# Rotary embedding over 16 heads: a skipped block of no-ops, and other cuts of the first load and the last stores

## The chip, the cores and the metric

The kernel runs on one core of a Trainium2 chip. A core has five engines with instruction streams of their own: TensorE (PE, matrix products, results in PSUM), VectorE (DVE), ScalarE (ACT), GpSimd (POOL) and SyncE (SP, which here only issues transfers). Data moves between the main memory and the on-chip memory (128 partitions) by 16 DMA engines; each has a ring of its own for every queue, and a DMA of 128 partitions is spread over all 16, eight partitions to each. The metric is the device time of one execution in microseconds; a smaller number is better.

## The reference

`x` is 16 x 512 x 1024 in float32 (33.5 MB), `cos` and `sin` are 512 x 32. Every row of 1024 is 16 heads of 64, and each head's two halves are rotated by the row's angles:

```python
x = x.reshape(batch, seq, num_heads, head_dim)
x1, x2 = x[..., :half_dim], x[..., half_dim:]
rotated = concatenate([x1 * cos - x2 * sin, x1 * sin + x2 * cos], axis=-1)
```

So every element is read once and written once: 67.1 MB in all.

## The kernel before

Two batch entries make one tile: 128 partitions, each with R = 8 consecutive rows of the sequence (32 KB). There are NT = 8 such tiles of 4 MB and NB = 5 buffers for them (`xin`), so tiles 5 to 7 reuse the buffers of tiles 0 to 2. A tile is computed in place and stored from its own buffer.

All loads and stores of tiles are issued by SP, on one queue, in this order: the first tile in four pieces of two rows (L64), tiles 1 to 4 whole, stores of tiles 0, 1, 2 (L69, each after its compute), loads of tiles 5, 6, 7 (each after the store that frees its buffer), then stores 3, 4, 5, 6 whole and store 7 in four pieces of two rows. SP is in order: what stands behind a waiting transfer waits too. The two tables go out on ScalarE's queue (sine L73, cosine L74).

At the head, GpSimd builds an identity (`ident`, L80 and L81), VectorE makes `sel` from it (L86 to L88), and TensorE spreads the two tables over 128 partitions with it (L93 to L95) into PSUM: `sns_ps` (minus sine and sine side by side) and `cos_ps`. ScalarE copies `sns_ps` to `sns` (L99), which GpSimd reads, and `cos_ps` to `cost` (L100), which nothing reads.

`compute(t)` is x times cosine plus the swapped halves of x times the signed sine:

- rows 0 and 1 (`PEROWS`): the sine product `B` (L126) is made by GpSimd for row 0 and by VectorE for row 1; VectorE multiplies the row by cosine in place (L136); TensorE adds the two in four chunks of 512 (L141, L142), and ScalarE copies each chunk back into the tile (L143).
- rows 2 and 3, 4 and 5, 6 and 7 (`PAIRS`): GpSimd makes the sine product `T` (L131, two buffers), VectorE makes the cosine product `pp` (L147) and adds the two into the tile (L148).

Each engine's order is the program's order (a manual schedule); semaphores carry what depends on another engine. A load piece is waited for by the instructions that read its rows: L126 and L136 by the first piece, L131 and L147 by the piece that holds their rows. A store piece waits for the instructions that wrote its rows.

Of the kernel before, what the change touches and what calls it, by code (L numbers as in the profile page):

```python
# [7 lines left out]
FP32 = mybir.dt.float32  # L8
# [4 lines left out]
def kernel(  # L13
# [8 lines left out]
    nc = tc.nc  # L22
    P = nc.NUM_PARTITIONS
    batch, seq, dim = x.shape
    nh = num_heads
    hd = dim // nh
    half = hd // 2
# [4 lines left out]
    R = seq // HP  # L32
    NT = batch // BP
    assert HP * R == seq and BP * NT == batch
    NB = 5
    PAIRS = (2, 4, 6)
    PEROWS = (0, 1)

    xv = x.rearrange("b (p r) d -> (b p) (r d)", r=R)
    xv = xv.rearrange("(t p) f -> t p f", p=P)  # L40
    ov = out.rearrange("b (p r) h d -> (b p) (r h d)", r=R)
    ov = ov.rearrange("(t p) f -> t p f", p=P)
# [3 lines left out]
    fixed = ctx.enter_context(tc.tile_pool(name="fixed", bufs=1))  # L46
# [8 lines left out]


    x_tiles = [None] * NT
    Q = 2 * dim

    def load(t, pieces=1):  # L60
        x_tiles[t] = xin.tile([P, R * dim], FP32, name="x_sb")
        n = R * dim // pieces
        for i in range(pieces):
            nc.sync.dma_start(out=x_tiles[t][:, i * n:(i + 1) * n], in_=xv[t][:, i * n:(i + 1) * n])  # L64

    def store(t, pieces=1):
        n = R * dim // pieces
        for i in range(pieces):
            nc.sync.dma_start(out=ov[t][:, i * n:(i + 1) * n], in_=x_tiles[t][:, i * n:(i + 1) * n])  # L69

    load(0, pieces=4)
    tabs = fixed.tile([HP, 2, R * half], FP32, name="tabs")
    nc.scalar.dma_start(out=tabs[:, 1], in_=sinv)  # L73
    nc.scalar.dma_start(out=tabs[:, 0], in_=cosv)  # L74
    for t in range(1, NB):
        load(t)


    ident = fixed.tile([P, P], FP32, name="ident")
    nc.gpsimd.memset(ident, 0.0)  # L80
# [1 line left out]
        out=ident, in_=ident, compare_op=ALU.not_equal, fill=1.0,  # L82
        base=0, pattern=[[-1, P]], channel_multiplier=1,
    )
    sel = fixed.tile([HP, 2, P], FP32, name="sel")
    nc.vector.tensor_copy(out=sel[:, 0, :HP], in_=ident[:HP, :HP])  # L86
    nc.vector.tensor_copy(out=sel[:, 0, HP:], in_=ident[:HP, :HP])
# [3 lines left out]
    cos_ps = ptab.tile([P, R, half], FP32, name="cos_ps")  # L91
# [3 lines left out]
    nc.tensor.matmul(out=cos_ps.rearrange("p r j -> p (r j)"), lhsT=sel[:, 0, :], rhs=tabs[:, 0],  # L95
                     start=True, stop=True)
    sns = fixed.tile([P, R, 2, half], FP32, name="sns")
    cost = fixed.tile([P, R, half], FP32, name="cost")
    nc.scalar.copy(out=sns, in_=sns_ps)  # L99
    nc.scalar.copy(out=cost, in_=cos_ps)  # L100

    def view(ap, r0, n):

        return ap[:, r0 * dim:(r0 + n) * dim]
# [5 lines left out]
    def snsb(tab, r0, n):  # L110
        return bass.AP(tensor=tab.tensor, offset=tab.offset + r0 * hd,
                       ap=[tab.ap[0], [hd, n], [0, nh], [1, hd]])

    def swapped(xt, r0, n):
        return bass.AP(tensor=xt.tensor, offset=xt.offset + r0 * dim + half,
                       ap=[xt.ap[0], [hd, n * nh], [-half, 2], [1, half]])

    def compute(t):
        xt = x_tiles[t]
        ts = {}  # L120
        bs = {}

        for r in PEROWS:
            B = bpool.tile([P, dim], FP32, name="B")
            eng = nc.vector if r == PEROWS[-1] else nc.gpsimd
            eng.tensor_tensor(out=B, in0=swapped(xt, r, 1), in1=snsb(sns_ps if eng is nc.vector else sns, r, 1),  # L126
                              op=ALU.mult)
            bs[r] = B
        for r0 in PAIRS:
            T = tpool.tile([P, 2 * dim], FP32, name="T")  # L130
            nc.gpsimd.tensor_tensor(out=T, in0=swapped(xt, r0, 2), in1=snsb(sns, r0, 2), op=ALU.mult)  # L131
            ts[r0] = T

        for r in reversed(PEROWS):
            xr = view(xt, r, 1)
            nc.vector.tensor_tensor(out=xr, in0=xr, in1=cosb(cos_ps, r, 1), op=ALU.mult)  # L136
            for c in range(2):
                ps = prow.tile([P, dim // 2], FP32, name="ps")
                xc = xr[:, c * dim // 2:(c + 1) * dim // 2]
                bc = bs[r][:, c * dim // 2:(c + 1) * dim // 2]  # L140
                nc.tensor.matmul(out=ps, lhsT=ident, rhs=xc, start=True, stop=False)  # L141
                nc.tensor.matmul(out=ps, lhsT=ident, rhs=bc, start=False, stop=True)  # L142
                nc.scalar.copy(out=xc, in_=ps)  # L143
        for r0 in PAIRS:
            pp = ppair.tile([P, 2 * dim], FP32, name="pp")
            xr = view(xt, r0, 2)
            nc.vector.tensor_tensor(out=pp, in0=xr, in1=cosb(cos_ps, r0, 2), op=ALU.mult)  # L147
            nc.vector.tensor_tensor(out=xr, in0=ts[r0], in1=pp, op=ALU.add)  # L148

    for t in range(NB):  # L150
        compute(t)
        if t < NT - NB:
            store(t)
    for t in range(NB, NT):
        load(t)
    for t in range(NT - NB, NB):
        store(t)
    for t in range(NB, NT):
        compute(t)
        store(t, pieces=4 if t == NT - 1 else 1)  # L160


# [33 lines left out]
```

## Time and profile before

| | |
|---|---|
| time, three runs | 162.82, 162.91, 163.51 us; median 162.91 |
| the profiled execution's own time | 162.99 us |
| its span, first to last instruction | 161.0 us (160.97) |
| VectorE busy | 137.8 us (86%), last instruction ends at 150.6 |
| GpSimd busy | 127.1 us (79%) |
| TensorE busy | 78.3 us (49%), mean granted clock 0.758 |
| ScalarE busy | 21.0 us (13%) |
| moved by DMA | 67.25 MB, 418 GB/s over the span |

Times within a profile count from the span's start. "Granted clock" is the share of TensorE's full speed that its throttle allowed. The page's "slices" cut the span in 40 and give each engine's busy share in tenths. In the DMA view a queue's row has its packets, megabytes, and the time that its packets took as a share of 16 engines' time; packets are counted where they start, so over a short window this can pass 100%. q1 is SP's queue, q10 ScalarE's, q14 that by which engines get their instructions. Behind the DMA view lie the records of single packets (start, length, size, queue); they don't name the DMA engine, but on a full ring each packet starts where the one before it ended, so a ring can be followed by its phase. In the timeline a row is: start, length, engine, line, operation, output<-inputs, forms, count, and in brackets the idle time before it and what ended it. An engine's name with a "q" is its instruction queue; a row "SPq" is the issue of DMAs.

### The profile page before, as it was taken

How to read it: one execution, taken by the hardware profiler on the slowest of the kernel's cores; microseconds unless marked ns; L12 is line 12 of the kernel's file. 1: busy time of each engine (PE TensorE's matmuls, PEld its weight loads, DVE VectorE, ACT ScalarE, POOL GpSimd, SP SyncE). 2: the span in 40 equal slices, each digit the busy share in tenths (PEclk: the TensorE clock that was granted, in tenths of full speed). 3: DMA queues.
4: the chain of work that ended last, by engine and by line, in shares of the span. 5: the costliest groups of instructions: out<-in, count | busy, mean ns of one | idle time of the engine just before them, and what ended most of it. 6: DMA issues, size and time to landing. Idle time of an engine off the chain costs nothing. (4 is left out here: it accounts for less than half of the span.)

```text
span 161.0 us, 581 instructions
## 1 busy us (share of the span) xinstructions
PE 78.3 (49%) x134; PEld 32.3 (20%) x134; DVE 137.8 (86%) x75; ACT 21.0 (13%) x35; POOL 127.1 (79%) x38
## 2 busy tenths in 40 slices
PE   0449900598019910894049700990079803991000
PEld 0223300233014400341024200340034202340000
DVE  1077999999999999999999999999999999999400
ACT  3021210014001210022002300121001400121000
POOL 1079999999998799959995999869995999692000
PEclk9999996569755985589957995699655975598555
DMA  5999999999999999999999999999999999999994
GB/s 181 385 419 480 391 497 415 391 472 440 391 456 456 391 432 480 391 415 489 399 417 472 407 415 464 415 407 472 423 399 456 448 399 456 448 391 417 421 423 187
DMA packets 3329, 67.25 MB, mean 418 GB/s; under 512 B 384, under 2 KB 512, under 8 KB 512
## 3 DMA queue, kind: packets, MB, share of 16 engines
q1 hardware_dynamic: 3168, 67.11, 97.6%
q10 hardware_dynamic: 160, 0.13, 0.3%
q14 instruction: 1, 0.01, 0.0%
HBM read 33.69 MB, written 33.55 MB: 418 GB/s over the span
## 5 line engine op out<-in xcount | busy, mean ns | idle before, releaser
L131 POOL TENSOR_TENSOR T<-x_sb,sns 128x2048 f32<-128x2048 f32 x24 | 108.2, 4526 | 10.5 <-DVE x_sb L148 10.5
L141 PE MATMUL ps<-x_sb,ident 128*128 128x512 f32 x64 | 44.8, 790 | 61.0 <-issue 40.4
L148 DVE TENSOR_TENSOR x_sb<-T,pp 128x2048 f32<-128x2048 f32 x24 | 54.9, 2288 | 3.4 <-POOL T L131 1.0
L147 DVE TENSOR_TENSOR pp<-x_sb,cos_ps 128x2048 f32<-128x2048 f32 x24 | 55.0, 2294 | 0.6
L142 PE MATMUL ps<-B,ident 128*128 128x512 f32 x64 | 40.3, 717 | 0.0
L143 ACT COPY x_sb<-ps 128x512 f32<-128x512 f32 x32 | 18.8, 586 | 117.6 <-PE ps L142 117.6
L141 PEld LDWEIGHTS ps<-x_sb,ident 128*128 128x128 f32 x64 | 15.2, 253 | 83.3 <-issue 80.4
L126 POOL TENSOR_TENSOR B<-x_sb,sns 128x1024 f32<-128x1024 f32 x8 | 18.8, 2346 | 7.6 <-ACT sns L99 7.6
L142 PEld LDWEIGHTS ps<-B,ident 128*128 128x128 f32 x64 | 15.4, 241 | 22.0 <-issue 22.0
L136 DVE TENSOR_TENSOR x_sb<-x_sb,cos_ps 128x1024 f32<-128x1024 f32 x16 | 18.8, 1218 | 0.5
L126 DVE TENSOR_TENSOR B<-x_sb,sns_ps 128x1024 f32<-128x1024 f32 x8 | 9.7, 1217 | 7.0 <-ACT sns L99 7.0
L93 PE MATMUL sns_ps<-tabs,sel 64*128 64x256 f32 x2 | 1.2, 697 | 6.2 <-DMA tabs<-in_sin_dram 6.2
L93 PEld LDWEIGHTS sns_ps<-tabs,sel 64*128 64x128 f32 x2 | 0.5, 310 | 6.1 <-issue 6.1
L99 ACT ACT_TABLE_LOAD x1 | 1.3, 1283 | 1.9 <-issue 1.9
L86 DVE COPY sel<-ident 64x64 f32<-64x64 f32 x1 | 0.2, 185 | 1.3 <-POOL ident L81 1.3
L99 ACT COPY sns<-sns_ps 128x512 f32<-128x512 f32 x1 | 0.6, 586 | 5.0 <-PE sns_ps L94 5.0
L95 PE MATMUL cos_ps<-tabs,sel 64*128 64x256 f32 x2 | 1.2, 711 | 0.0
L94 PE MATMUL sns_ps<-tabs,sel 64*128 64x256 f32 x2 | 1.1, 631 | 0.0
L94 PEld LDWEIGHTS sns_ps<-tabs,sel 64*128 64x128 f32 x2 | 0.7, 334 | 0.2
L95 PEld LDWEIGHTS cos_ps<-tabs,sel 64*128 64x128 f32 x2 | 0.5, 306 | 0.6 <-DMA tabs<-in_cos_dram 0.6
L100 ACT COPY cost<-cos_ps 128x256 f32<-128x256 f32 x1 | 0.4, 373 | 0.5 <-PE cos_ps L95 0.5
L80 POOL MEMSET ident<- 128x128 f32 x1 | 0.2, 204 | 0.3 <-POOLq L177 0.3
(7 smaller groups left out, 1.1 us busy)
## 6 DMA issues: line engine op xcount, KB each, us to landing
x_sb<-in_x_dram SPq DMA_DIRECT2D x7, 4096.0 KB, 29.5
out_dram<-x_sb SPq DMA_DIRECT2D x7, 4096.0 KB, 27.0
x_sb<-in_x_dram SPq DMA_DIRECT2D x4, 1024.0 KB, 8.7
out_dram<-x_sb SPq DMA_DIRECT2D x4, 1024.0 KB, 9.2
tabs<-in_sin_dram ACTq DMA_DIRECT2D x1, 64.0 KB, 5.3
tabs<-in_cos_dram ACTq DMA_DIRECT2D x1, 64.0 KB, 6.7
```

The source lines that it names most:

```text
L93: nc.tensor.matmul(out=sns_ps[:, :, 1, :], lhsT=sel[:, 0, :], rhs=sin3, start=True, stop=True)
L94: nc.tensor.matmul(out=sns_ps[:, :, 0, :], lhsT=sel[:, 1, :], rhs=sin3, start=True, stop=True)
L95: nc.tensor.matmul(out=cos_ps.rearrange("p r j -> p (r j)"), lhsT=sel[:, 0, :], rhs=tabs[:, 0], start=True, stop=True)
L99: nc.scalar.copy(out=sns, in_=sns_ps)
L126: eng.tensor_tensor(out=B, in0=swapped(xt, r, 1), in1=snsb(sns_ps if eng is nc.vector else sns, r, 1), op=ALU.mult)
L131: nc.gpsimd.tensor_tensor(out=T, in0=swapped(xt, r0, 2), in1=snsb(sns, r0, 2), op=ALU.mult)
L136: nc.vector.tensor_tensor(out=xr, in0=xr, in1=cosb(cos_ps, r, 1), op=ALU.mult)
L141: nc.tensor.matmul(out=ps, lhsT=ident, rhs=xc, start=True, stop=False)
L142: nc.tensor.matmul(out=ps, lhsT=ident, rhs=bc, start=False, stop=True)
L143: nc.scalar.copy(out=xc, in_=ps)
L147: nc.vector.tensor_tensor(out=pp, in0=xr, in1=cosb(cos_ps, r0, 2), op=ALU.mult)
L148: nc.vector.tensor_tensor(out=xr, in0=ts[r0], in1=pp, op=ALU.add)
```

## The change

- The first tile is loaded in two pieces, rows 0 and 1 (1 MB) and rows 2 to 7 (3 MB), instead of four of two rows. `load` and `store` now take the rows at which to cut.
- Stores 3, 4, 5 and 6 go out in two halves of four rows (2 MB each) instead of whole, and store 7 in two halves instead of four quarters. Stores 0 to 2 stay whole.
- On VectorE, ahead of its first work, a register is set to 0 and a branch on it skips 60 no-op instructions. In the built program the branch ends a block of instructions on every engine: each has an unconditional branch there (SP between the two pieces of the first load, ScalarE between the sine and the cosine load, GpSimd between L80's memset and L81's select, TensorE ahead of its first matmul), and VectorE has the compare-and-branch, the 60 no-ops and the branch behind them ahead of `sel`. No engine waits for another at these branches.
- The copy of `cos_ps` to `cost` is gone. Before, VectorE's first L136 waited for ScalarE (its copies); now it waits for TensorE.
- Two loads of tiles 3 and 4 had waited on SP for a semaphore of an earlier transfer to come free (for the sine load and for the first piece); with fewer pieces they no longer do.

```diff
+    PAD = 60
...
-    def load(t, pieces=1):
+    def load(t, cuts=(0, R)):
         x_tiles[t] = xin.tile([P, R * dim], FP32, name="x_sb")
-        n = R * dim // pieces
-        for i in range(pieces):
-            nc.sync.dma_start(out=x_tiles[t][:, i * n:(i + 1) * n], in_=xv[t][:, i * n:(i + 1) * n])
+        for a, b in zip(cuts, cuts[1:]):
+            nc.sync.dma_start(out=x_tiles[t][:, a * dim:b * dim], in_=xv[t][:, a * dim:b * dim])
 
-    def store(t, pieces=1):
-        n = R * dim // pieces
-        for i in range(pieces):
-            nc.sync.dma_start(out=ov[t][:, i * n:(i + 1) * n], in_=x_tiles[t][:, i * n:(i + 1) * n])
+    def store(t, cuts=(0, R)):
+        for a, b in zip(cuts, cuts[1:]):
+            nc.sync.dma_start(out=ov[t][:, a * dim:b * dim], in_=x_tiles[t][:, a * dim:b * dim])
 
-    load(0, pieces=4)
+    load(0, cuts=(0, 2, R))
...
+    step = nc.vector.alloc_register("step")
+    nc.vector.reg_mov(step, 0)
+    with tc.If(nc.vector.snap(step) > 0):
+        for _ in range(PAD):
+            nc.vector.nop(hint="pad")
...
-    cost = fixed.tile([P, R, half], FP32, name="cost")
     nc.scalar.copy(out=sns, in_=sns_ps)
-    nc.scalar.copy(out=cost, in_=cos_ps)
...
     for t in range(NT - NB, NB):
-        store(t)
+        store(t, (0, 4, R))
     for t in range(NB, NT):
         compute(t)
-        store(t, pieces=4 if t == NT - 1 else 1)
+        store(t, (0, 4, R))
```

More of the change, by code (lines that the diff above doesn't have):

```diff
@@ L57 @@
     x_tiles = [None] * NT
-    Q = 2 * dim
-    def load(t, pieces=1):
+    def load(t, cuts=(0, R)):
         x_tiles[t] = xin.tile([P, R * dim], FP32, name="x_sb")
-        n = R * dim // pieces
-        for i in range(pieces):
-            nc.sync.dma_start(out=x_tiles[t][:, i * n:(i + 1) * n], in_=xv[t][:, i * n:(i + 1) * n])
-    def store(t, pieces=1):
-        n = R * dim // pieces
-        for i in range(pieces):
-            nc.sync.dma_start(out=ov[t][:, i * n:(i + 1) * n], in_=x_tiles[t][:, i * n:(i + 1) * n])
-    load(0, pieces=4)
+        for a, b in zip(cuts, cuts[1:]):
[4 more added lines that the diff above has]
+    load(0, cuts=(0, 2, R))
     tabs = fixed.tile([HP, 2, R * half], FP32, name="tabs")
```

## Prediction

> **What bounds the kernel now.** I read the page's slices and queue table first, then the DMA view and the busy time by windows at the end, the chain of waits, and the timeline of the first 16 us and of the last tile. First the page (queue; packets, MB, share of 16 DMA engines over the span) and its slices:
>
> ```profile
> DMA  5999999999999999999999999999999999999994
> ...
> q1 hardware_dynamic: 3168, 67.11, 97.6%
> q14 instruction: 1, 0.01, 0.0%
> ```
>
> The transfers, all on one queue, fill the span: 0.976 of 161.0 us. In the packet records the first data packet starts at 1.74 us and the last ends at 159.81, and 97.6% of 160.97 us is 157.1 us, so hardly one microsecond of that stretch is idle. The page's chain of waits follows VectorE to its last instruction at 150.60; what remains, 10.4 us, is the drain of stores. The windows over that drain (DMA share is the last column but one):
>
> ```profile
> core 0: us, PE busy (x) PEld busy (x) DVE busy (x) ACT busy (x) POOL busy (x), PEclk, DMA share, GB/s
> 150.00:156.00 6.00, 0.00 (x0) 0.00 (x0) 0.60 (x1) 0.00 (x0) 0.00 (x0) 0.50 1.00 425
> ...
> 158.40:159.00 0.60, 0.00 (x0) 0.00 (x0) 0.00 (x0) 0.00 (x0) 0.00 (x0) 0.50 0.40 164
> 159.00:159.90 0.90, 0.00 (x0) 0.00 (x0) 0.00 (x0) 0.00 (x0) 0.00 (x0) 0.50 0.09 36
> ```
>
> Full until 158.4, then a tail of a few engines. The packet records show 14 DMA engines finishing at 158.43 to 158.96, one at 159.63, one at 159.81: the end is set by the slowest of 16 rings, each with a fixed share of the bytes. The last one has a history. In the DMA view of 82.0 to 82.3 us a packet of another queue stands in the stream:
>
> ```profile
> q14 instruction: 1, 0.01, 6.4%
> ```
>
> In the records it starts at 82.13 on the ring whose data packet ended at 82.13, takes 309 ns, and the 32 KB packet behind it takes 1745 ns instead of 1213: 0.31 + 0.53 = 0.84 us lost on one ring. Followed by its phase, that ring loses 0.385 us more in a packet at 109.67 (1598 ns), and is the one that ends at 159.81. Without the instruction packet it would have ended by 158.97.
>
> Then the compute at the head (start, length, engine, line, [idle before <- what ended it]):
>
> ```profile
> 8.05 1.22 PE L95 MATMUL cos_ps<-tabs,sel 64*128 64x256 f32 x2
> 8.86 1.22 DVE L126 TENSOR_TENSOR B<-x_sb,sns_ps 128x1024 f32<-128x1024 f32 x1 [6.99 <-ACT sns L99]
> ...
> 10.19 2.35 DVE L136 TENSOR_TENSOR x_sb<-x_sb,cos_ps 128x1024 f32<-128x1024 f32 x2
> 11.22 13.49 POOL L131 TENSOR_TENSOR T<-x_sb,sns 128x2048 f32<-128x2048 f32 x3
> ...
> 15.78 2.29 DVE L148 TENSOR_TENSOR x_sb<-T,pp 128x2048 f32<-128x2048 f32 x1 [1.03 <-POOL T L131]
> ```
>
> From 8.86 on VectorE works nearly without a gap (3.4 us idle at L148 in the whole run, page), so whatever delays the first L148 delays the end of compute by as much. And the last tile:
>
> ```profile
> 145.46 0.59 ACT L143 COPY x_sb<-ps 128x512 f32<-128x512 f32 x1 [1.13 <-PE ps L142]
> ...
> 146.08 2.26 SPq L69 DMA_DIRECT2D out_dram<-x_sb  x3
> 148.31 2.29 DVE L148 TENSOR_TENSOR x_sb<-T,pp 128x2048 f32<-128x2048 f32 x1
> ```
>
> Rows 0 and 1 are ready at 146.05, the last rows at 150.60; the rings are busy with the store before until 148.6 (fast rings) to 150.0 (the slow one). So the stores arrive in time, with 1 to 3 us to spare.
>
> **The change, part by part.**
>
> *Packets.* DMAs on the two queues: 24 before, 24 after. Per ring, 8 KB packets fall from 64 to 8, 8 of 24 KB and 80 of 16 KB come, 32 KB packets fall from 112 to 80. From the DMA view of 152 to 158 us (314 data packets, 101.4% of 16 x 6 us) an 8 KB packet is 310 ns; from that of 15 to 45 (400, 101.5%) a 32 KB one 1218. No 16 or 24 KB packet is in this trace; the straight line between those rows gives 613 and 915. Before 64 x 0.310 + 112 x 1.218 = 156.26 us; after 8 x 0.310 + 8 x 0.915 + 80 x 0.613 + 80 x 1.218 = 156.28. Bounds: at the 32 KB rate 609 ns, at the 8 KB rate 620 for 16 KB, so -0.4 to +0.7 us. I take the line: 0.0.
>
> *The first tile.* Its first piece is as before. The rest was 3 pieces landing at 8.9, 11.3 and 13.8 (issue plus the DMA view's time to landing: 1.16 + 7.7, 1.63 + 9.7, 2.10 + 11.7); now it is one, and lands with the last of those bytes, 13.8. GpSimd's first T (L131) needs rows 2 and 3: 11.22 becomes 13.80, +2.58. It takes 4.54, so VectorE's first L148 starts at 18.36, not 15.78. The later T's follow back to back as before, so the whole compute chain moves by 2.58: last L148 ends at 153.2. The cosine table is late too: in the records its 1 KB packets alternate one for one with the second piece's 8 KB packets (5.40 to 7.10 us), so with 24 KB packets five of them at 0.915 + 0.05 put it at about 5.1 + 4.8 = 9.9, plus 0.5 to the matmul at L95: 10.4 against 8.05. L136 then starts at 11.7 instead of 10.19 and ends at 14.0, its L147 at 16.3, before the 18.36: hidden behind the T. Who waits for the shifted compute: stores 0 to 2 on SP and the loads 5 to 7 queued behind them. Store 2 goes out at 65.3 instead of 62.7, while the rings hold store 1 until 71.2. Covered. Were that cover gone, 2.58 us would fall on the end.
>
> *The last tile.* The first half needs rows 0 to 3: ScalarE's last copy, 146.05 + 2.58 = 148.63, issue at 148.66. From issue to first packet I take 1.00 us (0.73 to 1.74 at the start of the run, the only time the rings were empty). It arrives at 149.66; the fast rings ran dry at 148.6 to 149.1, so they idle some 0.5 to 1.0 us. Their 16 packets of 613 ns then end at 149.66 + 9.81 = 159.47, still behind the slow ring at 159.63, which is dry only at 149.8. The second half is issued at 153.3 and needed at 154.6. So 0, with about 0.2 us left. ScalarE's chain length from L136 to the last copy's start is 10.1 to 11.5 us over the eight tiles (11.3 in the last), as the half-clock stretches fall, so the issue may come 1.2 us earlier or 0.3 later.
>
> *Halves for tiles 3 to 6.* They wait in the full queue behind loads 5 to 7; an earlier issue of a half moves nothing.
>
> *The no-ops.* The branch skips them (the register is 0). Its price is not in the trace; the nearest row is the branch that every engine already takes at L191: SP's last start semaphore is at 0.65, its first DMA at 0.73, so under 0.08 us. The far bound is a round trip of memory, the sine load's 5.3 us. VectorE idles 6.99 us before L126, and its sel work is needed at 6.13 and done at 1.87: 4.26 us of cover; even 5.3 us would start L126 1.0 us late, before the 2.58 that governs. On SP the branch stands between the two load pieces; the second must be issued by 4.73 - 1.00 = 3.7, and was at 1.16.
> [...]
>
> What the no-ops do move is where VectorE's instructions lie. At 82.13 VectorE was at its 63rd of 119 recorded instructions. If the packet at 82.13 was its own, 60 places more at the head put the same place of the program at the branch, before 1.74 us, when the rings are empty. I take that: the last ring falls from 159.81 to 158.97, and the end goes to the next, 159.63: -0.18. Bounds: 0 (another engine's packet), and -0.85 if that ring too joins the others.
>
> *The removed copy* (L100, 0.37 us on ScalarE): ScalarE waits 117.6 us for TensorE at L143; 0.
>
> **Sum.** 0.0 + 0 + 0 - 0.18 against the profiled execution: 162.99 - 0.18 = 162.8. That execution lies 0.08 above the median of 162.91, so 162.7 for a median.
>
> **Rivals.**
> 1. *The instruction packet stays in the stream* (not VectorE's, or it moves elsewhere): against it only the count of 63. Time 162.9 to 163.0.
> 2. *Slower: the last tile's first half comes too late for the rings.* End = issue + 1.00 + 9.81 + 0.35 (last packet to SP's semaphore) + 0.82 (to the span's end) + 2.02 (162.99 - 160.97) = issue + 14.00. At 148.66 that is 162.7; it decides from an issue of 148.8 (the 162.8 of the slow ring), and passes +0.5% (163.7) from 149.7. For it: the margin is tenths. At half clock a TensorE chunk takes 3.43 us against 1.72 (copies in the timeline); 5.7 us of the last chain ran at half clock, and a whole window of 10.24 us would add 2.3: 151.0, 165.0. Against: in eight tiles the chain never exceeded 11.5. Middle price 164.1.
> 3. *Faster: both slow rings join the others.* The end is then the fast rings', 158.97 if the first half comes at 147.5 (the short chain): 162.99 - 0.84 = 162.1, and 161.9 where the 14 end near 158.8. For it: the slow ring's excess is made of many small ones, not of its work. Against: the halves' wait usually costs the fast rings that much.
>
> **How the numbers follow.** Forecast 0.60 (162.7, own range 162.3 to 163.2), rival 1 0.13, rival 2 0.14, rival 3 0.13. About 0.5%, 0.8 us, is what a measurement of this kernel can tell from no change. Forecast and rival 1 lie within it: same 0.73; faster 0.13; slower 0.14. The range reaches to both sides' nearer cases: 161.9 to 163.8.
>
> **What would show it.** Right: the page's instruction packets gone from the stream or before 2 us; GpSimd's first L131 at 13.8; first L148 at 18.4; last L148 ending near 153.2; the last tile's first store issued 147.5 to 149.0; the last ring ending 159.4 to 159.7; span about 160.8. Wrong: idle DMA slices before 158, a gap on SP or VectorE of microseconds at the branch, 16 KB packets off 613 ns, or an issue after 149.7.

## The result, and the profile after

The changed kernel took 163.84 us (median of ten runs, 162.87 to 164.58) against 162.93 (ten, 162.82 to 163.51): ratio 1.0044, interval 1.0024 to 1.0064. It is slower, 0.04 us above the wider forecast range (161.9 to 163.8), and its runs scatter over 1.7 us where the kernel before stayed within 0.7 here (1.2 to 1.4 in the longer series of the experiments). The profiled execution took 164.43 us with a span of 162.14, so 1.17 us more inside the span than before and 0.27 more outside it (2.29 against 2.02). It is the second longest of the ten: their spans lie between 160.6 and 162.3 us, while what lies outside the span is 2.27 to 2.33 in all ten. So the 1.17 is that execution's, and at the median of the times the span has less of the loss.

The page's slices and queues of the changed kernel (queue; packets, MB, share of 16 engines), and below it a row of its DMA view for 5.1 to 5.4 us:

```profile
DMA  5999999999999999998998999998999999997993
...
q1 hardware_dynamic: 3168, 67.11, 97.1%
q14 instruction: 1, 0.01, 0.0%
```

```profile
q14 instruction: 1, 0.01, 7.3%
```

The instruction packet did move from 82.1 us to the head, but not into the empty time: it stands at 5.22 us, behind the eight packets of the first load piece on its ring, and in the middle of the stream. The packet records follow that ring by its phase: the 24 KB data packet behind it takes 1578 ns (elsewhere at most 1118), and the ring's part of the second load piece is done at 13.90, the next ring's at 13.23. At the first change from loads to stores its packet at 51.83 takes 1695 ns, against 1213 in the full stream, and it is done with the loads of the first five tiles at 53.52 (others 52.24 or earlier). At the second change, where the loads of tiles 5 to 7 end, its packet at 109.26 takes 1880 ns, and it is done at 112.35, the next at 110.48. It ends at 160.97, the fifteen others at 159.83 to 159.99.

The head (timeline rows: start, length, engine, line, idle time before and what ended it):

```profile
11.67 1.22 PE L101 MATMUL cos_ps<-tabs,sel 64*128 64x256 f32 x2 [3.21 <-DMA tabs<-in_cos_dram]
12.93 2.35 DVE L140 TENSOR_TENSOR x_sb<-x_sb,cos_ps 128x1024 f32<-128x1024 f32 x2 [2.59 <-PE cos_ps L101]
14.43 9.02 POOL L135 TENSOR_TENSOR T<-x_sb,sns 128x2048 f32<-128x2048 f32 x2 [2.92 <-DMA x_sb<-in_x_dram]
...
18.98 2.29 DVE L152 TENSOR_TENSOR x_sb<-T,pp 128x2048 f32<-128x2048 f32 x1 [1.50 <-POOL T L135]
```

The first T of GpSimd now waits for the load and starts 3.2 us later than before (11.22), VectorE's first add as much later (15.78). The last tile, and the windows over the drain (DMA share is the last column but one):

```profile
148.55 0.59 ACT L147 COPY x_sb<-ps 128x512 f32<-128x512 f32 x1 [1.13 <-PE ps L146]
149.16 5.00 SPq L67 DMA_DIRECT2D out_dram<-x_sb  x2
151.52 2.29 DVE L152 TENSOR_TENSOR x_sb<-T,pp 128x2048 f32<-128x2048 f32 x1
```

```profile
148.60:150.00 1.40, 0.00 (x0) 0.00 (x0) 1.37 (x2) 0.54 (x1) 0.37 (x1) 1.00 0.14 59
150.00:156.00 6.00, 0.00 (x0) 0.00 (x0) 3.70 (x2) 0.00 (x0) 0.00 (x0) 0.58 1.03 434
...
159.30:160.10 0.80, 0.00 (x0) 0.00 (x0) 0.00 (x0) 0.00 (x0) 0.00 (x0) 0.50 0.30 123
160.10:161.00 0.90, 0.00 (x0) 0.00 (x0) 0.00 (x0) 0.00 (x0) 0.00 (x0) 0.50 0.04 18
```

The first half of the last tile is issued at 149.16, and between 148.6 and 150.0 the rings are nearly empty (share 0.14): fifteen rings had finished the store before at 148.82 to 149.77 and get their next packet at about 150.0, most of them some 0.9 us later. But these end before 160.0. The last row (share 0.04) is one packet, on one ring: the late one sets the end.

### The profile page after: what moved, and what is told of

It is laid out like the page before. It is cut to its first block, busy times and chain, and to the rows that moved or that the text cites. A ratio compares the mean times of both kernels' runs of the same rounds, so it can differ in the third digit from the quotient of the medians.

```text
span 162.1 us, 583 instructions
## 1 busy us (share of the span) xinstructions
PE 77.7 (48%) x134; PEld 32.1 (20%) x134; DVE 137.8 (85%) x75; ACT 20.6 (13%) x34; POOL 127.1 (78%) x38
## 3 DMA queue, kind: packets, MB, share of 16 engines
q1 hardware_dynamic: 3168, 67.11, 97.1%
## 5 line engine op out<-in xcount | busy, mean ns | idle before, releaser
L135 POOL TENSOR_TENSOR T<-x_sb,sns 128x2048 f32<-128x2048 f32 x24 | 108.2, 4529 | 13.4 <-DVE x_sb L152 10.5
```

## The experiments

Two theories stood at the start: *late ring* (the end is set by the ring that took VectorE's instruction packet) and *late tail* (the compute, delayed by the 3 MB load piece, brings the last tile's halves too late). All ratios are to the kernel before on the same chip.

**1. Only the no-ops.**

```diff
+    PAD = 60
...
+    step = nc.vector.alloc_register("step")
+    nc.vector.reg_mov(step, 0)
+    with tc.If(nc.vector.snap(step) > 0):
+        for _ in range(PAD):
+            nc.vector.nop(hint="pad")
...
     sel = fixed.tile([HP, 2, P], FP32, name="sel")
```

> The kernel before with the 60 skipped no-ops on VectorE and nothing else changed. Late-ring theory (the end is set by the one DMA ring that took VectorE's instruction packet; at 5.2 us it loses 0.7 us there, and more at each change of the stream from loads to stores): the packet stands near 5 us, the last ring ends 160.3 to 161.0 while the others end near 158.9, time 163.4 to 164.2. Late-tail theory (the 3 MB load piece delays the compute, and halves of the last tile then reach the rings too late): neither is here, so 162.9, as before, and the last ring no later than 159.8.

163.54 us (162.82 to 164.48) against 163.04; ratio 1.0039, 1.0019 to 1.0060. The instruction packet stands at 4.98 (DMA view of 4.9 to 5.2 us):

```profile
q14 instruction: 1, 0.01, 6.4%
```

Compute is as before (last VectorE instruction ends at 150.6), so the late tail is out for this loss. One ring is 0.5 us behind the next at 13.7 and 1.0 behind at 111.5 (111.50 against 110.47), and ends at 160.04 in the profiled execution, the next at 159.35. The profiled execution (163.35) is one of the lower of its twelve; its last ring is 0.3 us short of the expected 160.3. The ring accounts only for what lies inside the span: the mean span of the twelve is 161.40 us against 161.12, +0.28, while time less span is 2.29 against 2.00, +0.29 (2.11 to 2.68; three of the twelve lie above 2.5). This second half of the loss, neither theory had.

**2. Only the cuts** (the changed kernel without the branch and the no-ops).

```diff
-    step = nc.vector.alloc_register("step")
-    nc.vector.reg_mov(step, 0)
-    with tc.If(nc.vector.snap(step) > 0):
-        for _ in range(PAD):
-            nc.vector.nop(hint="pad")
```

> The changed kernel without the no-ops and their branch: only the cuts of loads and stores and the missing copy. Late-ring theory: the instruction packet is back near 82 us, one ring loses 0.8 us there and is hit at one change to stores instead of two; first L148-line add at 18.3; last ring 159.6 to 160.2, the others 159.4 to 159.8, time 162.8 to 163.2. Late-tail theory: 163.6 to 163.9, as changed.

163.52 (163.35 to 163.80); ratio 1.0031, 1.0020 to 1.0042. Inside the span the late-ring theory holds: the packet is back at 84.67, last ring at 159.89, next 159.45, first add of the pairs at 18.25, last VectorE instruction ends at 153.07, first half of the last tile issued at 148.07. The mean span is 161.23 us against 161.12. But the time is higher than that: time less span is 2.29 (2.25 to 2.34 in seven runs) against 2.00. So 0.3 of the 0.48 us lie outside the span, which neither theory had.

**3. Thirty no-ops.** As experiment 1, with `PAD = 30`.

> The kernel before with 30 skipped no-ops instead of 60. If the packet at 82 us is VectorE's, it moves to about the time when VectorE reaches its 31st recorded instruction of the kernel before, some 30 to 46 us, give or take the rings' backlog of some us; one ring then meets two changes to stores (52 and 110 us) after the loss: last ring 160 to 161, time 163.2 to 164.2. If it is another engine's, the packet stays near 82 us and the time at 162.9.

163.85 (163.71 to 164.42); ratio 1.0059, 1.0039 to 1.0079. The packet stands at 42.08 (DMA view of 42.0 to 42.3 us):

```profile
q14 instruction: 1, 0.01, 6.8%
```

82 us with none, 42 with 30, 5 with 60: the packet is VectorE's, shown. The 32 KB data packet behind it took 1867 ns. That ring is then hit at both changes to stores (packets of 1709 ns at 51.67 and 1962 at 109.05) and ends at 160.77, the next at 159.28. Here the loss lies inside the span: its mean is 161.88 us against 161.12 (+0.76), time less span 2.08 against 2.00. Nothing in the profile but the late ring accounts for it; the compute ends at 151.0, before the rings need it.

**4. One no-op.** As experiment 1, with `PAD = 1`.

> The kernel before with one skipped no-op: the branch and the cut of every engine's program into blocks, without the distance. Both theories: the instruction packet within some us of 82, time 162.8 to 163.1 as before. If the branch itself costs something (a stall at the head), sel on VectorE would be made after 6 us and the time would rise.

163.06; ratio 0.9998, 0.9986 to 1.0011; packet at 82.22. The branch and the cut into blocks cost nothing that can be measured; the distance does (30 no-ops 1.0059, 60 no-ops 1.0039).

**5. Only the copy gone, 6. only the load cut, 7. only the stores cut.**

```diff
-    cost = fixed.tile([P, R, half], FP32, name="cost")
...
-    nc.scalar.copy(out=cost, in_=cos_ps)
```
```diff
-    load(0, pieces=4)
+    load(0, cuts=(0, 2, R))
```
```diff
-        store(t)
+        store(t, (0, 4, R))
...
-        store(t, pieces=4 if t == NT - 1 else 1)
+        store(t, (0, 4, R))
```

> The kernel before without ScalarE's copy of cos_ps, nothing else. In the cuts-only run 0.3 us of the loss lay outside the span (time less span 2.29 against 2.00 before) and 0.1 inside. Theory: the length of an engine's program sets when it fetches its last instructions behind the end, and ScalarE's is one shorter here: time less span 2.2 to 2.4, time 163.2 to 163.4, span as before (161.1). Rival: it is SP's or GpSimd's program that counts, or the way the stores end: nothing here, 2.00 and 163.0.

> The kernel before with the first tile loaded as rows 0-1 and 2-7; stores and copy as before, no no-ops. Both theories of the time inside the span: first add of the pair rows at 18.3 instead of 15.8, last VectorE instruction at 153.1, cosine matmul near 10.5 to 11.5; the instruction packet 2.5 us later than before, near 84.7. Late-ring theory: last ring near 159.8 as before, time 162.9 to 163.2, the four quarters being small enough for the later compute. Late-tail theory (compute 2.5 us later costs by itself): last ring 160.3 or later, time 163.4 or more.

> The kernel before with stores 3 to 7 in halves of four rows; load in quarters and copy as before, no no-ops. The compute ends at 150.6 as before, so both halves of the last tile are issued before the rings need them (146.1 and 150.6). Late-ring theory: as before, 162.9 to 163.2, last ring 159.6 to 160.0, instruction packet at 82. If halves by themselves cost (16 KB packets slower than 613 ns), all rings end later, 159.5 or more. If SP's three more instructions set what lies outside the span, time less span is 2.2 to 2.4 here instead of 2.0.

| | time | ratio | mean span | time less span |
|---|---|---|---|---|
| before, same chip | 163.03 | 1 | 161.12 | 1.95 |
| copy gone | 163.03 | 1.0004, 0.9987 to 1.0020 | 161.03 | 2.05 |
| load cut | 163.22 | 1.0013, 0.9999 to 1.0026 | 161.08 | 2.17 |
| stores cut | 163.27 | 1.0014, 0.9998 to 1.0029 | 161.30 | 2.02 |

None is resolved by itself. The load cut delays the compute as forecast (last VectorE instruction ends at 152.97) and leaves the span alone. Of what lies outside the span it has 0.2 us, the copy 0.1, the stores 0.07: together 0.4, where experiment 2 had 0.3. The expectation that the copy alone explains it fell.

**8 and 9. A ring made late by hand, at the head or near the end.** ScalarE issues one load of 16 KB into one partition, to put one packet on one ring; its data is not used.

```diff
     nc.scalar.dma_start(out=tabs[:, 0], in_=cosv)
+    late = fixed.tile([1, 4096], FP32, name="late")
+    nc.scalar.dma_start(out=late, in_=xv[0][0:1, 0:4096])
```

In experiment 9 the load stands behind the compute of tile 6 instead:

```diff
         compute(t)
+        if t == 6:
+            nc.scalar.dma_start(out=late, in_=xv[0][0:1, 0:4096])
```

> The kernel before, and one extra packet put on a single ring at the head: ScalarE issues a load of 16 KB into one partition behind the cosine load; its data is not used. The instruction packet stays at 82. Late-ring theory (a ring that is late, for whatever reason, loses again when the stream changes from loads to stores): one ring 0.6 to 1.2 us late from about 8 us, 0.4 to 0.7 more near 51 and near 110, last ring 160.3 to 161.5, time 163.5 to 164.6. Rival (the growth belongs to instruction fetching itself): the ring stays 0.6 late, hidden behind the ring of the instruction packet, 162.9 to 163.2.

> The same 16 KB packet on one ring, issued by ScalarE after its copies for tile 6, near 128 us, when only stores follow. Late-ring theory: the ring is 0.6 to 1.2 us late and loses nothing more; unless it is the ring that is late already, last ring 159.6 to 160.2 and time 162.9 to 163.3, less than with the packet at the head by 0.4 or more. Rival (a packet costs the same wherever it stands): the same time as with the packet at the head.

163.29, ratio 1.0008 (0.9990 to 1.0026), and 163.15, ratio 0.9991 (0.9970 to 1.0011). Inconclusive for the time: at the head the ring became 0.6 us later than the middle one, as expected, but only 0.2 later than the next (8.59 against 8.38), and it stayed hidden behind the ring of the instruction packet in both. What the first profile does show is that this ring lost nothing more at the first change (0.2 behind the next at 42.7, 0.2 at 52.6), as the rival said. So not every late ring loses there.

**10. Marks on the rings.** Fifteen loads of 64 bytes to 1, 2, ... 15 partitions on ScalarE's queue behind the first tile; data not used.

```diff
+    marks = fixed.tile([16, 16 * 16], FP32, name="marks")
...
     for t in range(NB):
         compute(t)
+        if t == 0:
+            for n in range(1, 16):
+                nc.scalar.dma_start(out=marks[0:n, n * 16:(n + 1) * 16], in_=xv[0][0:n, n * 16:(n + 1) * 16])
```

> The kernel before with fifteen small loads (64 bytes to each of 1, 2, ... 15 partitions, data not used) on ScalarE's queue after the first tile, which put 15 small packets on the first ring, one fewer on each next. Neither theory gives a time (ScalarE is held up by their issue, some us). It shows which ring has the instruction packet and which is slow besides: if the slow one besides is always the same ring, its lag is that ring's own, and is not noise.

166.63 in one run. The marks disturbed what they were to read, through SP's waits:

```profile
SPq L64 <- DMA marks<-in_x_dram: 27.6, 1, 27.6
```

SP issued the loads of tiles 3 and 4 only at 33.81 and 34.18 (before: both by 6.85), because, by the profile, it waited 27.6 us for one of the marks to land. Meanwhile the rings ran out of work:

```profile
31.00:32.40 1.40, 1.40 (x3) 0.67 (x2) 1.40 (x2) 0.00 (x0) 1.40 (x2) 0.50 0.87 375
32.60:34.20 1.60, 1.60 (x3) 0.67 (x2) 1.50 (x2) 0.00 (x0) 1.60 (x1) 0.50 0.00 0
34.20:36.00 1.80, 1.80 (x4) 0.53 (x2) 1.77 (x2) 0.00 (x0) 1.80 (x1) 0.73 1.06 292
```

Which ring is slow besides wasn't settled, nor was it shown that the first ring had fifteen of the marks and each next one fewer, which was the author's assumption: ScalarE's queue has 400 packets against 160 in the kernel before, two for each of the 120 partitions loaded, and no packet's ring is recorded.

**11. Three such packets before the first change to stores.** As 8, and again behind the compute of tiles 0 and 1.

```diff
     for t in range(NB):
         compute(t)
+        if t < 2:
+            nc.scalar.dma_start(out=late, in_=xv[0][0:1, 0:4096])
```

> The kernel before, and the 16 KB packet to one partition three times before the first change of the stream to stores: at the head, and by ScalarE behind its copies for tile 0 and for tile 1 (about 8, 22 and 42 us). In the run with one packet its ring was an early one and the packet made it late by only 0.2 us against the others. Now it is 1.4 to 2.0 us late at 51 us. Late-ring theory (a late ring loses again at a change from loads to stores): 0.4 to 0.7 more at 51 to 53 us and at 109 to 112, its end at 160.9 to 162, time 163.9 to 165.2. Rival (the growth belongs to the ring that carries instructions): no growth, the ring ends where the three packets put it, 160.0 to 160.5, time 163.1 to 163.6.

164.63 (164.23 to 164.99); ratio 1.0096, 1.0062 to 1.0130. The ring is 1.4 us behind the next at 44.1, and at the first change its packet at 51.37 takes 1720 ns instead of some 1215: 54.30 against 52.38. At the second change it loses nothing more. It ends at 160.98, the others by 159.59. The mean span is 162.65 us against 161.17 (+1.48), time less span 1.97 against 2.02: all of the loss is inside. So the time follows one late ring, and a ring made late by data alone can lose half a microsecond more at the first change; in experiment 8, with a lag of 0.6 us to the middle ring, it didn't. Being late isn't a condition for it either: in experiment 2 fifteen packets around the first change took 1314 to 1881 ns, most of them on rings that weren't late. Growth at the second change was seen only on rings that had taken instructions, and not on all of them (not here, on the ring of the packet at 82.2).

**12. No-ops, and the first load held back until VectorE is past them.** A column of the first tile is written by VectorE ahead of the load, which then overwrites it; `made=True` has the load use the tile that is there.

```diff
+    PAD = 60
...
-    def load(t, pieces=1):
-        x_tiles[t] = xin.tile([P, R * dim], FP32, name="x_sb")
+    def load(t, pieces=1, made=False):
+        if not made:
+            x_tiles[t] = xin.tile([P, R * dim], FP32, name="x_sb")
...
-    load(0, pieces=4)
+    step = nc.vector.alloc_register("step")
+    nc.vector.reg_mov(step, 0)
+    with tc.If(nc.vector.snap(step) > 0):
+        for _ in range(PAD):
+            nc.vector.nop(hint="pad")
+    x_tiles[0] = xin.tile([P, R * dim], FP32, name="x_sb")
+    nc.vector.memset(x_tiles[0][:, 0:1], 0.0)
+    load(0, pieces=4, made=True)
```

> The kernel before with the 60 skipped no-ops, and the first load held back until VectorE is past them (a write of one column of the first tile by VectorE, which the load then overwrites). Late-ring theory: the instruction packet finds empty rings and stands before the first data packet; no ring is late from it; the stream starts 0.5 to 1.0 us later than 1.74, the last ring is the slow one besides, 159.6 plus that, time 163.0 to 163.6 with less scatter than with the no-ops alone (162.8 to 164.5 there), and the tables land before 5 us. Rival (the no-ops cost by themselves, wherever the packet stands): 164 and the same scatter. If the packet still waits behind the first piece: 164 to 165.

164.08 (163.76 to 164.51); ratio 1.0060, 1.0036 to 1.0083. The packet is at 2.58, before the first packet of a tile (2.91), and no ring is late: at 109 to 112 us the last is 0.15 behind the fourteenth, at the end 160.04 against 159.89. The drain's windows of this run:

```profile
158.40:159.30 0.90, 0.00 (x0) 0.00 (x0) 0.00 (x0) 0.00 (x0) 0.00 (x0) 0.50 0.97 410
159.30:160.10 0.80, 0.00 (x0) 0.00 (x0) 0.00 (x0) 0.00 (x0) 0.00 (x0) 0.50 0.30 123
160.10:161.00 0.90, 0.00 (x0) 0.00 (x0) 0.00 (x0) 0.00 (x0) 0.00 (x0) 0.50 0.00 0
```

Full to the end, with no tail of one ring. This shows one half of the mechanism: here a packet that met a ring without tiles (2.58 against 2.91) made no ring late. That the time then falls back is not shown. It came out at the rival's 164, though not with the rival's scatter (0.75 us here, 1.7 in experiment 1), and most of the loss lies outside the span: time less span is 2.56 in the mean (2.28 to 2.74) against 2.02, the mean span 161.54 against 161.17. Two things went up inside the span: the first piece is done 1.0 us later (6.17 against 5.14 for the fourteenth ring), and all rings lost some 0.8 us at the first change to stores (the tile that ends there takes 10.5 us instead of 9.7). So a cost of the skipped no-ops outside the span, wherever their packet stands, isn't excluded: experiment 1 has 0.3 us there too, experiment 3 0.1.

## Why the prediction was wrong

- **Packets: right.** In the changed kernel's window of 115 to 148 us, 871 data packets of 16 KB took 101.0% of 16 x 33 us: 612 ns against 613 taken. (The lower bound of this term, by its own rates, is -0.3 and not -0.4 us.)
- **The first tile: right in mechanism, 0.6 us short.** The T was put at 13.80 and the add at 18.36; with the cuts alone they came at 13.70 and 18.25. In the changed kernel 14.43 and 18.98, because the whole 3 MB piece waits for the one late ring (done at 13.90, the next at 13.23), which this step didn't have. The cosine matmul came at 11.67, not 10.4: the one-for-one alternation was right, but the 24 KB packets took 960 ns (median; 915 taken), and the table was done on fifteen rings by 10.50 and on the late one at 11.15.
- **The last tile: right in size.** Issue at 149.16 (148.66 plus the 0.6 above, less a shorter chain), first packet 0.84 later (1.00 taken), fast rings at 159.83 to 159.99 (159.47 said). It was not what ended last.
- **The no-ops' instruction packet: the step that failed.** "I take that: the last ring falls from 159.81 to 158.97, and the end goes to the next, 159.63: -0.18. Bounds: 0 ... and -0.85". The move to the head was right, and VectorE's count of 63 named the right engine (experiment 3). Wrong was "before 1.74 us, when the rings are empty": it took the time of the branch for the time of the packet and put the cost of a packet at the head at nothing, and so bounded the term on one side only. The sine load stood in the same profile as a warning: issued at 0.73, its packets run at 4.69, behind the first piece. The packet came at 5.22, and a ring late from the head passes two changes to stores instead of one: it ended at 160.97, +1.34 against the 159.63 taken. That is the profiled execution; for the median time of 163.84 the same way back (2.30 outside the span, 1.17 from the last packet to the span's end, in both profiles) puts the last ring at about 160.4, an estimate, so +0.7. With the no-ops alone (experiment 1) the mean span is 0.28 us longer and the time 0.5.
- **Outside the span: a term the sum didn't have.** 2.02 us was carried over; it is 2.29 in the profiled execution, +0.27, and 2.30 in the mean of the ten. The two add up: 162.8 + 1.34 + 0.27 = 164.4, the profiled 164.43.
- **The branch itself: right.** One no-op: 0.9998. With 60, in the changed kernel, the compare-and-branch takes 56 ns, VectorE's first copy behind it starts at 1.47 us (1.33 before), and SP's second load piece goes out at 1.17 (1.16 before); in experiment 12 VectorE is past it by 1.52. The far bound of 5.3 us was the author's estimate, from the sine load's time to landing; no run shows such a wait at the branch. Nor did VectorE wait for its instructions later: in the profile before it is busy for the whole of 82 to 84 us (2.00 of 2.00), around the packet at 82.13, while the DMA ring that carried the packet lost 0.84 us.
- **The rivals.** The late tail was real on fifteen rings and hidden by the sixteenth. That a ring's lateness could grow was not among them, though the profile before had it: 0.84 lost at 82, 0.385 more at 109.67.

Open: why rings lose time at a change to stores, and a late one often more; why the load cut, and the no-ops, lengthen what lies outside the span; and why the runs scatter. A guess for the last, from the profiles, is that a ring's loss at the changes differs from run to run (0.0 to 0.75 us in them).

## What to carry to other kernels

In both kernels here the DMA engines are full nearly from end to end (97.6 and 97.1% of the span on SP's queue), and the span is set by the slowest of sixteen rings: in the changed kernel the last ends at 160.97, the others by 159.99. Where a kernel looks like that, look at the last windows of the drain and follow that ring back: with the 8 KB packet of instructions at 42 us instead of 82 (experiment 3) the mean span is 0.76 us longer. An instruction moved ahead of a stream needn't move its transfer there: in the changed kernel the branch is at 0.91 us and the first data packet at 1.75, and the transfer stands at 5.22, behind what the ring already had. And a lone late ring can cost more than its first loss when changes from loads to stores still lie ahead of it: in experiment 11 one that was 1.4 us behind the next at 44.1 is 1.9 behind at the first change. By the place of the instruction packet, the mean span is 161.1 with it at 82 us, 161.9 at 42, 161.4 at 5.

## What the runs showed of the hardware

- The packet records show sixteen rings and more than one queue on each: in the changed kernel the 128 packets of the first load piece run eight to a ring (8 KB each), then those of the second eight to a ring (24 KB each), all of SP's queue; between the 24 KB packets stand 1 KB packets of ScalarE's queue, 46 ns each at the median, the last at 10.19 us. Besides its data each of the 24 DMAs has 16 packets of 4 bytes, 384 in all.
- An instruction packet of 8 KB cost its ring 0.84 to 0.99 us between 32 KB packets (309 or 325 ns, and a following packet of 1745 to 1875 instead of 1213), and about 0.46 between 8 KB packets: in experiment 11, with three more DMAs on ScalarE, a second one stands in the span, at 149.29, and the 8 KB packet behind it took 465 ns instead of 309.
- In the kernel before the next instruction packet stands just behind the span (1.05 us after its end), and 0.5 to 0.7 us later in the three kernels without ScalarE's copy. What lies outside the span doesn't simply follow it: with only the copy gone the packet is the latest of the three (1.79 us after the end) and time less span is 2.05; with only the load cut it stands at 1.03 and time less span is 2.17.
- In experiment 10 the order of the waits on one queue emptied all rings: fifteen loads of 8 KB in all, on another engine's queue, kept SP from issuing two tiles for 27.6 us, and no packet of a tile started from 32.6 to 34.2 us.
